# Bias rows two heads ahead on the ACT queue, and stores moved from POOL to ACT, in a two-layer decoder step

## The chip, the cores and the metric

One core of one Trainium2 chip runs the whole program. The metric is the device time in microseconds (us) of one execution, given as the median of several runs. Engines are named as in the profile: PE (TensorE matmul) and PEld (its weight load), DVE (VectorE), ACT (ScalarE), POOL (GpSimd), SP (SyncE, which here only issues DMAs). Each engine works through its own instructions in the order written. A DMA is issued by an instruction of SP, ACT or POOL; one that has to wait for data holds everything that is queued behind it on that engine.

## The reference, cut to what matters

One inference step of a two-layer decoder, on a prompt of 256 tokens and 8 samples of 8 tokens each (N = 320 columns), with width 2048, all in float32:

```python
# layer 0 (even): one input projection, two branches, one output projection
z = x @ w_in                               # 73 column tiles of 128
qa, ka, va, ga, qm, km, vm, om, gm, im, fm = split(z)
attn = moba(qa, ka, va, rel_bias)          # 8 heads of 128; prompt: causal softmax(q k^T*scale + T5 bias) v
                                           # samples: 16 cached pages of 128 keys each, top 3 blocks of 256 + own keys
hm, state = mlstm(qm, km, vm, im, fm)      # 4 heads of 256, matrix memory C, normaliser n, stabiliser m
x = layernorm(ALPHA*x + concat(attn*silu(ga), headnorm(hm)*sigmoid(om)*silu(gm)) @ w_out)
# layer 1 (odd): y = w_out(B * conv3(C * (w_in x)) * silu(G)), then layernorm again
```

Besides the two x, it returns the keys and values of layer 0 (`k_out`, `v_out`), the mLSTM's final states (`cp_out` for the prompt, `cs_out`, `n_out`, `m_out`) and the convolution's last rows. The T5 bias of a prompt head depends only on the distance between query and key.

## The kernel before, in words

All activations are kept transposed, 128 features by 320 columns. A projection tile is `lin`: 128 output columns, weights in two halves of 512 KB (`raw`, 11 buffers, loaded on SP at L226). ACT copies a half to float32r (`sh`) and DVE makes the remainder (`sl`, both by the helper at L202 to L204, recorded as L86); PE then does 24 matmuls per half from `sh` and `sl`. At most 4 halves are split ahead (`HL`). Attention over the cached pages uses the same `raw` buffers: each item loads two pages, one on SP and one on POOL (`k_load` L456, `v_load` L464), and goes to PE unsplit (`kv`).

The order of work is written out when the program is built. Items (weight halves, page pairs, mLSTM states) stand in one list: 8 page items, then 4 or 5 weight halves, and so on. Between matmuls, `stages()` steps four `Chain` queues of generators (A: sample softmax, B and E: prompt heads, values, mLSTM; C: gates) when a small model (`Plan`) says that the time has come. The model prices PE, ACT and DVE instructions, and no DMA issue.

Prompt attention, per head h: the key tile (`post_k`, L350) is evacuated by ACT (`kT`) and DVE (`ks`) and stored by two DMAs on POOL; the value tile (`post_v`, L359) is evacuated by ACT and stored by one DMA on POOL; then `prompt_head` (L404) is put on chain B (even h) or E (odd h). It loads `bt`, 128 rows of 256 bias values that are windows of the DRAM row `rel` (L406, on POOL), does the scores on PE, and DVE adds the bias (L413, L414). Row maxima on DVE, exponentials on ACT, a scaling on DVE and transposes on PE follow. `bt` has two buffers.

`rel` is made once by `bias_rows` (L324): one PE product, one DVE addition, one store on POOL (L330), and 8 small loads of `dt15` from it, on POOL too (L333).

The mLSTM (`mlstm_head`, L832, on chain B) reads weighted keys `ml.ks` and values `ml.vs` made by `k_natural` and `vm_natural`; these were written to DRAM (`kd`, `vd`) by 4 + 4 DMAs of POOL at L803 and L829 and are read back some hundred us later by `new_states` (L1252). `cp_out` is stored at L942 on POOL.

Of the kernel before, what the change touches and what calls it, by code (L numbers as in the profile page):

```python
# [18 lines left out]
F32 = mybir.dt.float32  # L19
# [9 lines left out]
T = 256  # L29
# [4 lines left out]
AH = 8  # L34
# [25 lines left out]
def _rev(ap, first, n):  # L60

    return bass.AP(tensor=ap.tensor, offset=ap.offset + first, ap=[list(ap.ap[0]), [-1, n]])
# [88 lines left out]
def trunk_kernel(ctx, tc, x_in, kc, vc, pages, cst_in, seg_in, hot_in, small_in, c0_in, n0_in, w_in,  # L151
                 y_out, k_out, v_out, cp_out, cs_out, n_out, m_out, conv_out):
    nc = tc.nc
# [4 lines left out]
    def mm(out, lhsT, rhs, tiles=1, **k):  # L158

        n = math.prod(rhs.shape[1:])  # L160
        cost = max(n * 1.68e-3, 0.21) if rhs.dtype == F32 else max(n * 0.46e-3, 0.11)
        plan.t -= 0.2
        plan.spend("pe", cost / tiles, 0.2)
        nc.tensor.matmul(out, lhsT=lhsT, rhs=rhs, **k)  # L164

    def transpose(out, in_, identity):
        plan.t -= 0.2
        plan.spend("pe", 0.22, 0.2)
        nc.tensor.transpose(out, in_, identity)  # L169
# [135 lines left out]
    ks = pa_.tile([128, AH, 64], F32, name="ks")  # L305
# [9 lines left out]
    p1_ = p1.__enter__()  # L315
    qT = M[:, 8:16, 0:T]
    kT = p1_.tile([128, AH, T], F32, name="kT")
# [4 lines left out]
    rel = dr.tile([8, 512], F32, name="rel")  # L322

    def bias_rows():  # L324
        r = b_bank()
        mm(r[:8, :512], lhsT=small[:32, S_REL:S_REL + 8], rhs=hot[:, :512], start=True, stop=True)
        yield HOLD
        row = early[:8, 1024:1536]
        dve.tensor_tensor(row, r[:8, :512], hot[:8, 512:1024], op=OP.add)
        nc.gpsimd.dma_start(rel, row)  # L330
        for hf in range(2):
            for j in range(4):
                nc.gpsimd.dma_start(dt15[32 * j:32 * j + 32, hf, :],  # L333
                                    bass.AP(tensor=rel.tensor, offset=rel.offset + 512 * (4 * hf + j) + 120,
                                            ap=[[0, 4], [1, 8], [1, 136]]))

        dve.tensor_tensor(om[:, 4:8], onb[:, 0:4], onb[:, 4:8], op=OP.add)
        dve.tensor_scalar(om[:, 4:8], om[:, 4:8], 1.0, -NEG, op0=OP.subtract, op1=OP.mult)
        yield
# [10 lines left out]
    def post_k(h):  # L350
        def f(p):
            act(kT[:, h, :], p[:, :T], AF.Copy)
            dve.tensor_copy(ks[:, h, :], p[:, T:])
            nc.gpsimd.dma_start(k_out[h][:, 0:T], kT[:, h, :])
            nc.gpsimd.dma_start(k_out[h][:, T:], ks[:, h, :])
            k_seen[0] += 1
        return f

    def post_v(h):  # L359
        def f(p):  # L360
            if h >= 2:
                B.until(f"v{h - 2}")
            v = p1_.tile([128, N], F32, name="vstage", tag="vstage", bufs=2)
            act(v, p, AF.Copy)
            nc.gpsimd.dma_start(v_out[h], v)
            B.add_urgent(f"v{h}", v_natural(h, v))
            (B, E)[h % 2].add(f"attn{h}", prompt_head(h, (b_bank, c_bank)[h % 2]))
        return f

    def v_natural(h, v):  # L370
        yield
        t = b_bank()
        transpose(t[:, 0:128], v[:, 0:128], ident)
        transpose(t[:, 128:256], v[:, 128:256], ident)
        transpose(t[:64, 256:384], v[:, 256:320], ident)
        yield HOLD
        c = slice(h * 128, h * 128 + 128)
        act(vp[:, :, h, :], t[:, :256].rearrange("p (j d) -> p j d", j=2), AF.Copy)
        dve.tensor_copy(vs[:, c], t[:64, 256:384])
        yield  # L380
# [15 lines left out]
    def post_ga(h):  # L396
        def g(p):
            sg = gate_tile()
            yield from sigmoid(p, sg)
            dve.tensor_tensor(M[:, h, :], p, sg, op=OP.mult)  # L400

        return lambda p: C.add(f"post{cga[h]}", g(p))

    def prompt_head(h, x_bank):  # L404
        bt = p1_.tile([128, 256], F32, name="bt", tag="bt", bufs=2)
        nc.gpsimd.dma_start(bt, bass.AP(tensor=rel.tensor, offset=rel.offset + 512 * h, ap=[[1, 128], [1, 256]]))  # L406
        s = x_bank()
        mm(s[:, 0:128], lhsT=qT[:, h, 0:128], rhs=kT[:, h, 0:128], start=True, stop=True)
        mm(s[:, 128:384], lhsT=qT[:, h, 128:256], rhs=kT[:, h, 0:256], start=True, stop=True)
        yield HOLD  # L410
        S = p1_.tile([128, 384], F32, name="pS", tag="pS", bufs=2)
        st4 = p1_.tile([128, 8], F32, name="st4", tag="st4", bufs=2)
        dve.scalar_tensor_tensor(S[:, 0:128], s[:, 0:128], SCALE, _rev(bt, 127, 128), op0=OP.mult, op1=OP.add)  # L413
        dve.scalar_tensor_tensor(S[:, 128:384], s[:, 128:384], SCALE, _rev(bt, 255, 256), op0=OP.mult, op1=OP.add)  # L414
        dve.tensor_reduce(st4[:, 0:1], S[:, 0:128], axis=AX.X, op=OP.max, negate=True)
        dve.tensor_reduce(st4[:, 1:2], S[:, 128:384], axis=AX.X, op=OP.max, negate=True)
        yield
        act(S[:, 0:128], S[:, 0:128], AF.Exp, bias=st4[:, 0:1], accum_out=st4[:, 2:3])
        act(S[:, 128:384], S[:, 128:384], AF.Exp, bias=st4[:, 1:2], accum_out=st4[:, 3:4])
        yield  # L420
        dve.reciprocal(st4[:, 4:6], st4[:, 2:4])
        dve.tensor_scalar(S[:, 0:128], S[:, 0:128], st4[:, 4:5], None, op0=OP.mult)
        dve.tensor_scalar(S[:, 128:384], S[:, 128:384], st4[:, 5:6], None, op0=OP.mult)
        yield
        t = x_bank()
        for j in range(3):
            transpose(t[:, j * 128:j * 128 + 128], S[:, j * 128:j * 128 + 128], ident)
        yield HOLD
        P = p1_.tile([128, 384], F32, name="pP", tag="pP", bufs=2)
        act(P, t[:, :384], AF.Copy)  # L430
        yield
        B.until(f"v{h}")
        o = x_bank()
        mm(o[:, 0:256], lhsT=vp[:, 0, h, :], rhs=P[:, 0:256], start=True, stop=False, skip_group_check=True)
        mm(o[:, 128:256], lhsT=vp[:, 1, h, :], rhs=P[:, 256:384], start=False, stop=True, skip_group_check=True)
        yield HOLD
        while f"post{cga[h]}" not in C.done:
            yield HOLD
        dve.tensor_tensor(M[:, h, 0:T], o[:, 0:256], M[:, h, 0:T], op=OP.mult)
        yield  # L440
# [198 lines left out]
    ml = ML()  # L639
    ml.states = -1  # L640
    ml.dec = pc.tile([128, 32], F32, name="dec")
    kd, vd = (dr.tile([BH, 4, 64, DK], F32R, name=n) for n in ("kd", "vd"))
# [144 lines left out]
    def k_natural(hd, kt):  # L787
        yield
        t = b_bank()
        for j, (c, n) in enumerate(TOK):  # L790
            transpose(t[:n, j * 128:j * 128 + 128], km[hd][:, kt, c:c + n], ident)
        yield HOLD
        c = slice(kt * 128, kt * 128 + 128)
        w = lambda j: ml.AT[:TOK[j][1], j, 4 + hd:5 + hd]
        act(ml.ks[:64, c], t[:64, 256:384], AF.Identity, scale=w(2))
        for j in range(2):
            act(ml.kw[:, j, c], t[:, j * 128:j * 128 + 128], AF.Identity, scale=w(j))
        yield HOLD
        dve.scalar_tensor_tensor(ml.ks[64:128, c], t[:64, 256:384], w(2), ml.ks[:64, c].bitcast(F32),
                                 op0=OP.mult, op1=OP.subtract)  # L800
        if kt == 1:
            for r in range(4):
                nc.gpsimd.dma_start(kd[hd, r], ml.ks[64 * (r // 2):64 * (r // 2) + 64, :])  # L803
        yield

    def post_vm(hd, kt):
# [8 lines left out]
    def vm_natural(hd, v, kt):  # L815
        yield
        t = b_bank()
        for j, (c, n) in enumerate(TOK):
            transpose(t[:n, j * 128:j * 128 + 128], v[:, c:c + n], ident)
        yield HOLD  # L820
        c = slice(kt * 128, kt * 128 + 128)
        act(ml.vs[:, 0, c], t[:64, 256:384], AF.Copy)
        act(ml.vn[:, 0:2, c], t[:, 0:256].rearrange("p (j c) -> p j c", j=2), AF.Copy)
        yield HOLD
        act(ml.vn[:64, 2, c], t[:64, 256:384], AF.Copy)
        dve.tensor_tensor(ml.vs[:, 1, c], t[:64, 256:384], ml.vs[:, 0, c].bitcast(F32), op=OP.subtract)
        if kt == 1:
            for r in range(4):
                nc.gpsimd.dma_start(vd[hd, r], ml.vs[:, r % 2, :])  # L829
        yield  # L830

    def mlstm_head(hd):  # L832
# [31 lines left out]
        if hd == BH - 1:  # L864
            nc.gpsimd.dma_start(n_out, ml.n0)
        B.done.add(f"qw{hd}")
        yield
        t = b_bank()
        for kt in range(2):
# [64 lines left out]
        cp = P2.tile([128, 2, 258], F32, name="cp", tag="hn")  # L934
        for kt in range(2):
# [3 lines left out]
            yield HOLD  # L939
            act(cp[:, kt, :], t[:, :258], AF.Copy)  # L940
            yield
        nc.gpsimd.dma_start(cp_out[hd], cp)  # L942
        yield

    def rsqrt_step(y, var, t):
# [699 lines left out]
```

## Time and profile before

| | before |
|---|---|
| median of 3 runs | 1482.01 us (1481.88 to 1488.57) |
| profiled execution | 1483.53 us, span 1481.9 us |
| PE busy | 1446.9 us, 98% of the span |
| DVE, ACT, POOL busy | 774.7, 599.7, 265.2 us |
| DMA | 356.45 MB, 241 GB/s over the span |

Layer 0's input projection with both attentions and the mLSTM takes the first 770 us or so; output projection, layer 1 and the closing norm take the rest. The page counts a matmul as busy from its issue to a modelled end, so PE at 98% is not PE at its full rate; PEclk is the share of the full clock (2.4 GHz) that was granted, the lower of the two levels being 1.2 GHz.

### The profile page before, as it was taken

What the parts mean: (1) busy time and instruction counts of PE and PEld (TensorE: products, weight loads), DVE (VectorE), ACT (ScalarE), POOL (GpSimd) and SP (SyncE); (2) the same over time, 40 slices, a digit from 0 to 9 for tenths busy, and PEclk for the clock granted to TensorE, in tenths of its full rate; (3) what the DMA queues carried; (4) which work ended last, traced back from release to release, by engine and by line L of the source; (5) the groups of instructions that cost most, each with busy time, mean ns of one, the idle gap of its engine ahead of it and who ended that gap; (6) DMA issues with size and microseconds to landing.
All of it is one profiled execution on the core that took longest, in us unless ns stands there. A gap on an engine that the chain in (4) does not pass through costs nothing.

```text
span 1481.9 us, 32269 instructions
## 1 busy us (share of the span) xinstructions
PE 1446.9 (98%) x11983; PEld 1376.5 (93%) x11983; DVE 774.7 (52%) x1296; ACT 599.7 (40%) x1124; POOL 265.2 (18%) x500
## 2 busy tenths in 40 slices
PE   9999998799999999999999999999999999999998
PEld 9799888798889789899899999999999999999998
DVE  5324424234333433433457766776776666666665
ACT  5335434234333343433455343444443334334344
POOL 1422212113212232222101025313110000000000
PEclk9999999899999999999999999999999999999999
DMA  9889878758999998998954657767665444444412
GB/s 358 308 306 346 295 274 293 260 198 286 343 323 338 333 344 286 353 335 275 367 221 160 197 164 221 230 227 230 208 217 171 153 143 144 154 143 159 147 41 71
DMA packets 134575, 356.45 MB, mean 241 GB/s; under 512 B 24453, under 2 KB 30854, under 8 KB 134418
## 3 DMA queue, kind: packets, MB, share of 16 engines
q1 hardware_dynamic: 94082, 258.53, 50.3%
q0 software_dynamic: 40336, 95.87, 18.9%
q8 instruction: 94, 1.54, 0.4%
q14 instruction: 63, 0.52, 0.1%
HBM read 337.31 MB, written 16.98 MB: 239 GB/s over the span
## 4 chain that ended last, share of the span: by engine, by line
PE 78%; DMA 8%; issue 6%; DVE 2%; POOL 2%; POOLq 1%; ACT 1%; SPq 0%; ACTq 0%; DVEq 0%
PE lin L164 67%; PE kv L164 6%; DMA raw<-w_all 4%; DMA bt<-rel 2%; PE mB L164 2%; PE mC L164 2%; DVE sl L86 1%; POOLq L454 1%; ACT sh L86 1%; PE mB L169 1%; DMA pt<-pages 1%; PE mA L169 0%; POOL raw L461 0%; POOL Xl L1263 0%; DVE M L86 0%
## 5 line engine op out<-in xcount | busy, mean ns | idle before, releaser
L86 DVE TENSOR_TENSOR sl<-raw,sh 128x1024 fp32r<-128x1024 f32 (+1 forms) x341 | 410.5, 1214 | 387.9 <-ACT sh L86 377.7
L164 PE MATMUL lin<-Xh,sh 128*128 128x320 f32 x1648 | 524.6, 318 | 3.3 <-DVE sg L86 2.0
L164 PE MATMUL lin<-Xh,sl 128*128 128x320 f32 x1648 | 511.9, 311 | 1.4 <-DVE sl L86 1.4
L164 PE MATMUL lin<-Xl,sh 128*128 128x320 f32 x1648 | 511.9, 311 | 0.0
L86 ACT ACTIVATE sh<-raw 128x1024 fp32r<-128x1024 f32 (+1 forms) x341 | 352.9, 1046 | 318.8 <-PE lin L164 118.0
L164 PEld LDWEIGHTS lin<-Xh,sh 128*128 128x128 f32 x1648 | 312.0, 189 | 15.7 <-issue 5.5
L164 PE MATMUL lin<-X2h,sh 128*128 128x322 f32 x1024 | 318.6, 311 | 0.0
L164 PE MATMUL lin<-X2l,sh 128*128 128x322 f32 x1024 | 318.0, 311 | 0.0
L164 PE MATMUL lin<-X2h,sl 128*128 128x322 f32 x1024 | 317.8, 310 | 0.0
L164 PEld LDWEIGHTS lin<-Xh,sl 128*128 128x128 f32 x1648 | 311.6, 189 | 2.0 <-DVE sl L86 1.9
L164 PEld LDWEIGHTS lin<-Xl,sh 128*128 128x128 f32 x1648 | 312.1, 189 | 0.9 <-DVE Xl L86 0.3
L164 PEld LDWEIGHTS lin<-X2l,sh 128*128 128x128 f32 x1024 | 193.9, 189 | 0.1
L164 PEld LDWEIGHTS lin<-X2h,sh 128*128 128x128 f32 x1024 | 192.9, 188 | 0.1
L164 PEld LDWEIGHTS lin<-X2h,sl 128*128 128x128 f32 x1024 | 192.6, 188 | 0.0
L461 POOL DMA_DIRECT2D raw<-kc x128 | 69.0, 539 | 209.5 <-PE kv L164 73.8
L469 POOL DMA_DIRECT2D raw<-vc x128 | 68.9, 539 | 206.7 <-PE kv L164 85.2
L164 PE MATMUL kv<-raw,qp 128*32 128x256 f32 x1024 | 61.5, 382 | 2.5 <-DMA raw<-kc 1.4
L164 PE MATMUL kv<-raw,PT 128*32 128x128 f32 x2048 | 61.0, 274 | 0.0
L164 PEld LDWEIGHTS kv<-raw,PT 128*32 128x32 f32 x2048 | 54.7, 110 | 5.5 <-issue 4.6
L164 PEld LDWEIGHTS kv<-raw,qp 128*32 128x32 f32 x1024 | 30.5, 110 | 25.0 <-issue 5.4
L1290 POOL DMA_DIRECT2D cs_o<-xr x32 | 17.7, 552 | 158.2 <-DVE xr L86 158.2
L1350 POOL DMA_DIRECT2D conv_o<-ncv x1 | 0.5, 539 | 218.3 <-ACT ncv L86 218.3
(313 smaller groups left out, 1105.2 us busy)
## 6 DMA issues: line engine op xcount, KB each, us to landing
raw<-w_all SPq DMA_DIRECT2D x335, 512.0 KB, 4.6
raw<-kc POOLq DMA_DIRECT2D x128, 256.0 KB, 5.8
raw<-kc SPq DMA_DIRECT2D x128, 256.0 KB, 6.2
raw<-vc SPq DMA_DIRECT2D x128, 256.0 KB, 5.9
raw<-vc POOLq DMA_DIRECT2D x128, 256.0 KB, 6.0
raw<-c SPq DMA_DIRECT2D x32, 256.0 KB, 6.7
xr<-c POOLq DMA_DIRECT2D x32, 256.0 KB, 4.8
cs_o<-xr POOLq DMA_DIRECT2D x32, 256.0 KB, 4.5
```

Of the source, the lines that this page charges most:

```text
L86: return fn(out, *a, **k)
L164: nc.tensor.matmul(out, lhsT=lhsT, rhs=rhs, **k)
L169: nc.tensor.transpose(out, in_, identity)
L454: return queue.value_load(pt[0:1, b * NPG + j:b * NPG + j + 1], min_val=0, max_val=NPOOL - 1)
L461: queue.dma_start(r[:, j, :], kc[bass.ds(n, 1), u.half].rearrange("o p f -> (o p) f"))
L469: queue.dma_start(r[:, j, :], vc[bass.ds(n, 1), :, 512 * u.half:512 * u.half + 512] .rearrange("o p f -> (o p) f"))
L1290: nc.gpsimd.dma_start(cs_out[hd, b], c)
L1350: nc.gpsimd.dma_start(conv_out, ncv)
```

## The change

`bias_load(h)` takes the place of the load at the head of `prompt_head`. The loads for heads 0 and 1 are issued at the end of `bias_rows`' DMAs; the load for head h + 2 is issued right after DVE's two additions of head h (which read the buffer that it overwrites). They are issued by ACT instead of POOL. The stores of keys, values and `cp_out` are issued by ACT too. The writes of `kd` and `vd` stay on POOL and move from the ends of `k_natural` and `vm_natural` to `mlstm_head`, behind the step that makes `qw`.

```diff
@@ bias_rows
+        for h in range(2):
+            bias_load(h)
@@ post_k, post_v
-            nc.gpsimd.dma_start(k_out[h][:, 0:T], kT[:, h, :])
-            nc.gpsimd.dma_start(k_out[h][:, T:], ks[:, h, :])
+            nc.scalar.dma_start(k_out[h][:, 0:T], kT[:, h, :])
+            nc.scalar.dma_start(k_out[h][:, T:], ks[:, h, :])
-            nc.gpsimd.dma_start(v_out[h], v)
+            nc.scalar.dma_start(v_out[h], v)
@@ prompt_head
+    bts = {}
+
+    def bias_load(h):
+        if h < AH:
+            bts[h] = p1_.tile([128, 256], F32, name="bt", tag="bt", bufs=2)
+            nc.scalar.dma_start(bts[h], bass.AP(tensor=rel.tensor, offset=rel.offset + 512 * h, ap=[[1, 128], [1, 256]]))
+
     def prompt_head(h, x_bank):
-        bt = p1_.tile([128, 256], F32, name="bt", tag="bt", bufs=2)
-        nc.gpsimd.dma_start(bt, bass.AP(tensor=rel.tensor, offset=rel.offset + 512 * h, ap=[[1, 128], [1, 256]]))
+        bt = bts.pop(h)
...
         dve.scalar_tensor_tensor(S[:, 128:384], s[:, 128:384], SCALE, _rev(bt, 255, 256), op0=OP.mult, op1=OP.add)
+        bias_load(h + 2)
@@ k_natural, vm_natural
-        if kt == 1:
-            for r in range(4):
-                nc.gpsimd.dma_start(kd[hd, r], ml.ks[64 * (r // 2):64 * (r // 2) + 64, :])
-        if kt == 1:
-            for r in range(4):
-                nc.gpsimd.dma_start(vd[hd, r], ml.vs[:, r % 2, :])
@@ mlstm_head
         B.done.add(f"qw{hd}")
+        for r in range(4):
+            nc.gpsimd.dma_start(kd[hd, r], ml.ks[64 * (r // 2):64 * (r // 2) + 64, :])
+            nc.gpsimd.dma_start(vd[hd, r], ml.vs[:, r % 2, :])
...
-        nc.gpsimd.dma_start(cp_out[hd], cp)
+        nc.scalar.dma_start(cp_out[hd], cp)
```

## Rows read from the trace of the kernel before

**Rows 1.** The page's chain that ended last, by line.
```profile
PE lin L164 67%; PE kv L164 6%; DMA raw<-w_all 4%; DMA bt<-rel 2%; PE mB L164 2%; PE mC L164 2%; DVE sl L86 1%; POOLq L454 1%; ACT sh L86 1%; PE mB L169 1%; DMA pt<-pages 1%; PE mA L169 0%; POOL raw L461 0%; POOL Xl L1263 0%; DVE M L86 0%
```

**Rows 2.** Busy time by stretch: length, PE, PEld, DVE, ACT, POOL, clock, DMA.
```profile
180.00:340.00 160.00, 142.19 (x1409) 131.73 (x1407) 56.72 (x107) 57.69 (x121) 34.94 (x65) 0.94 0.73 261
...
360.00:760.00 400.00, 395.32 (x4161) 356.07 (x4154) 154.90 (x312) 154.91 (x319) 97.34 (x181) 1.00 0.92 329
780.00:880.00 100.00, 100.00 (x682) 99.84 (x682) 71.39 (x109) 46.29 (x69) 9.12 (x23) 1.00 0.55 180
```

**Rows 3.** Waits of PE from 120 to 340 us: total, times, longest.
```profile
PE mB L169 <- DVE pS L86: 9.3, 1, 9.3
PE mC L169 <- DVE pS L86: 7.5, 2, 4.5
```

**Rows 4.** Waits of DVE in the same stretch.
```profile
DVE pS L86 <- DMA bt<-rel: 50.5, 7, 13.5
```

**Rows 5.** Chain of waits around the bias loads of heads 4 and 6: start, length, what.
```profile
225.32 4.64 DMA raw<-w_all
...
288.12 7.35 DMA bt<-rel
295.56 0.62 DVE pS L86 x2
...
297.97 0.95 PE mB L169 x3
```

**Rows 6.** The tile bt: issue duration (ns), first and last start; landing times.
```profile
L406 POOL DMA_DIRECT2D bt<-rel x8: 536/536/545, 121.2 to 322.7; - x8
L86 DVE SCALAR_TENSOR_TENSOR pS<-mB,bt x8: 283/352/415, 130.2 to 295.8; 128x128 f32<-128x128 f32 x4, 128x256 f32<-128x256 f32 x4
...
DMA to landing us min/median/max: 5.5/6.8/9.1
```

**Rows 7.** Busy time by stretch, where the granted clock was low.
```profile
180.00:200.00 20.00, 16.99 (x106) 16.43 (x104) 7.60 (x14) 7.26 (x16) 2.68 (x5) 0.91 0.75 270
...
260.00:300.00 40.00, 30.70 (x286) 29.27 (x286) 9.83 (x18) 10.04 (x20) 6.46 (x12) 0.84 0.64 234
300.00:320.00 20.00, 20.00 (x232) 18.59 (x232) 7.77 (x10) 7.52 (x11) 4.84 (x9) 0.91 0.60 204
```

**Rows 8.** Timeline of ACT, 42 us: the query copies of the first page unit.
```profile
42.46 0.35 ACT L86 ACTIVATE qp<-qs 128x32 f32<-128x32 f32 x2 [0.24 <-DVE qs L86]
```

**Rows 9.** Timeline of DVE, 43 us: the addition that makes the row rel.
```profile
43.42 0.67 DVE L86 TENSOR_TENSOR S<-mB,S 8x512 f32<-8x512 f32 x1
```

**Rows 10.** Chain of waits at 44 us.
```profile
44.38 2.10 DMA rel<-S
```

**Rows 11.** Timeline of PE: the first page bunch, and waits in the second.
```profile
44.55 3.66 PE L164 MATMUL kv<-raw,qp 128*32 128x256 f32 x64 [1.01 <-issue]
...
66.56 0.64 PE L164 MATMUL kv<-raw,qp 128*32 128x256 f32 x8 [0.79 <-DMA raw<-kc]
67.79 0.64 PE L164 MATMUL kv<-raw,qp 128*32 128x256 f32 x8 [0.59 <-DMA raw<-kc]
```

**Rows 12.** Timeline of SP: a lone issue, and seven stores issued one behind another.
```profile
11.53 0.31 SPq L1107 DMA_DIRECT2D pt<-pages  x1
...
1475.96 3.45 SPq L1522 DMA_DIRECT2D y_o<-M  x7
```

**Rows 13.** Timeline of POOL: a store of keys and a write of kd that waited.
```profile
309.47 0.54 POOL L354 DMA_DIRECT2D k_o<-kT  x1 [20.82 <-ACT kT L86]
...
562.94 1.07 POOL L803 DMA_DIRECT2D kd<-kws  x2 [8.49 <-ACT kws L86]
```

**Rows 14.** Timeline of DVE, then of ACT: qw of mLSTM head 0, next write of vms.
```profile
402.62 0.22 DVE L86 TENSOR_TENSOR qw<-qm,mB 128x64 f32<-128x64 f32 x1 [0.16 <-ACT dt L86]
...
467.35 0.27 ACT L86 ACTIVATE vms<-mB 64x128 fp32r<-64x128 f32 x1 [3.45 <-PE mB L169]
```

**Rows 15.** The page's groups of instructions: the splits of DVE and ACT.
```profile
L86 DVE TENSOR_TENSOR sl<-raw,sh 128x1024 fp32r<-128x1024 f32 (+1 forms) x341 | 410.5, 1214 | 387.9 <-ACT sh L86 377.7
L86 ACT ACTIVATE sh<-raw 128x1024 fp32r<-128x1024 f32 (+1 forms) x341 | 352.9, 1046 | 318.8 <-PE lin L164 118.0
```

## The prediction

> **What bounds the kernel now.** I read the chain of waits first. It runs through PE for most of the span, but one transfer stands in it that moves no weights: the bias rows, 2% of the span [rows 1]. The busy times by stretch say where that hurts. From 360 to 760 us PE is idle 400 - 395.32 = 4.68 us, from 780 to 880 us it is never idle; from 180 to 340 us it is idle 160 - 142.19 = 17.81 us, and the granted clock is 0.94 there against 1.00 in the others [rows 2]. So the first layer's prompt heads hold the only large loss. PE's own waits in that stretch name it: three times its transposes wait for DVE's `pS`, 9.3 + 7.5 = 16.8 us together [rows 3]. DVE in turn waited 50.5 us, at seven of the eight heads, for `bt` [rows 4]. The chain around head 6 shows the link: load issued at 288.12, DVE's addition at 295.56, PE's transposes at 297.97 [rows 5]. The load is issued only when its head begins and takes 5.5 to 9.1 us to land [rows 6], while the plan, which prices no DMA, has already put the transposes into PE's order.
>
> **Bias rows two heads ahead.** On one chain the additions of heads 0 and 6 start at 130.2 and about 295.5 us, so two heads lie some 55 us apart [rows 5, 6]. Issued right behind head h, a load that needs 5.5 to 9.1 us has landed long before head h + 2, even if the stretch shrinks by 20 us. The DVE wait goes for all seven heads. What is late next is PE's normal work: the stretch from 360 us on has the same mix of weights and pages without bias waits, and loses 4.68 us in 400, which is 1.9 in 160 [rows 2]. Idle time saved: 17.8 - 1.9 = 15.9 us. Its bounds are 0, if another wait takes all of it, and 17.8.
>
> The clock comes back too. Granted shares of 0.91, 0.84 and 0.91 over 20, 40 and 20 us [rows 7] lack 1.8 + 6.4 + 1.8 = 10 us of full clock, that is 20 us at 1.2 GHz instead of 2.4, each time around an idle PE. Where PE was idle at the low level it lost nothing more; if all idle time fell there, only 10 - 17.8/2 = 1.1 us of work was lost, if none did, 10. I take 6, near the middle, since the clock is still low in a stretch where PE is busy for all of its 20 us [rows 7].
>
> DMA must follow. The stretch moved 261 GB/s over 160 us, 41.8 MB. Pressed into 138 us that is 303 GB/s, below the 329 GB/s kept up from 360 to 760 us [rows 2], so I cost it at 1 us.
>
> **The first two loads.** They cost something. `bias_rows` is stepped before the first page unit's query copies, so on ACT the loads for heads 0 and 1 stand in front of the two `qp` copies that ran at 42.46 us [rows 8]. The loads read `rel`, which DVE makes at 43.42 [rows 9], and whose store lands at 44.38 + 2.10 = 46.48 [rows 10]. ACT is held until then, issues two DMAs and copies for 0.35 us. Behind it waits PE: the first 64 page matmuls started at 44.55 and need `qp` [rows 11].
>
> No DMA is issued by ACT in this trace. The nearest rows are SP's: 0.31 us alone, and 3.45/7 = 0.49 us in a row [rows 12]. I take 0.45, with 0.31 and POOL's 0.54 [rows 6] as ends. So PE starts at 46.48 + 0.9 + 0.35 = 47.7, which is 3.2 us later. The clock may dip behind that pause as it did near the others: 1.8 us at most, taken from the stretch at 180 [rows 7]; I take 1.5. In return, the second bunch of pages, for which PE waited 0.79 + 0.59 = 1.4 us [rows 11], has landed when PE comes to it, since POOL's loads don't hang on `qp`. Net cost 3.2 + 1.5 - 1.4 = 3.3 us, with bounds 0 and 5.
>
> A rule of the Trainium skill bears on the 0.45: Perfetto Trace Analysis, "DMA Instruction — HWDGE (DVE, Sync)", says that the sequencers issuing hardware-generated DMAs share one descriptor generator and wait for its lock. No run here shows it, as SP alone issues such DMAs. By it, each of the two loads could also wait out one of SP's issues, about 0.5 us each as an estimate from the rows above, and the forecast would be 1 us higher.
>
> **Stores and loads on ACT.** ACT issues 16 key stores, 8 value stores, 8 bias loads and 4 `cp_out`: 36 x 0.45 = 16.2 us. ACT is busy 154.91 of 400 us [rows 2], so most of it lies in idle time. The waits matter more. The second key store waits for DVE's `ks`, and the load for head h + 2 waits for DVE's additions of head h; behind them on ACT stand the splits `sh`, for these DVE's `sl`, and for that PE. With up to four halves split ahead, I cost this at 1 us; if the cover is gone, the bound is the second rival below. The value stores and `cp_out` wait for ACT's own copies only.
>
> **POOL.** It loses 36 issues of 0.54 us and waits such as the 20.82 us in front of a key store [rows 13]. The page loads behind these start earlier, but SP loads the other page of each pair and the buffers come free no sooner; apart from the 1.4 us counted above I give this nothing, with 0 and 2 us as bounds.
>
> **kd and vd.** The eight writes of a head move to where their data is long made, so waits such as 8.49 us [rows 13] leave POOL. The next head overwrites `vms` no sooner than 467.35, and the writes now start near 402.62 [rows 14]; eight issues of 0.54 us and a landing of some us fit into those 65 us. Cost and gain 0, within 1 us either way. `cp_out` likewise.
>
> **The sum**, against the profiled execution of 1483.53 us (span 1481.9, and 1.6 around it): -15.9 - 6 + 1 + 3.3 + 1 = -16.6, so 1466.9. The median of the runs shown lies 1.5 lower, at 1482.01; from it I forecast 1465 us, with 1460 to 1471 as the likeliest case's own range.
>
> **Rivals.**
> *Late weights take the wait's place.* Behind a bias wait the chain shows a weights load of 4.64 us whose slot had only been freed by DVE after that wait [rows 5]. If such a load, not the bias, is next at each of the three heads where PE stalled, 3 x 4.64 = 13.9 us of the gain come back: 1479 us. For it: DMA is near 92% later on. Against it: the slot comes free earlier when DVE isn't held.
> *ACT and DVE in lock step.* Slower. Eight bias loads and eight key stores hold ACT until DVE has caught up. Then a split starts only after the hold, and PE gets its half one ACT copy and one DVE remainder late: 1.046 + 1.214 = 2.26 us [rows 15], sixteen times 36 us. The time would be 1465 + 36 - 1 = 1500. It beats the gain once (16.6 + 1)/16 = 1.1 us of each hold reaches PE. For it: DVE's idle time is mostly a wait for `sh`, 377.7 us [rows 15]. Against it: up to four halves lie ready, and heads come some 27 us apart.
> *The loads come no earlier.* If ACT reaches them so late that DVE still waits, nothing is gained and the start costs 3.3: 1485 us. The 55 us between heads speak against it.
> *More than forecast.* The pause at 44 us is hidden and all 10 us of clock return: 1482 - 15.9 - 10 + 1 = 1457 us.
>
> **Chances.** Forecast 0.64, late weights 0.14, lock step 0.10, no earlier 0.04, more 0.08. The range from 1456 to 1480 takes in the first, the second and the last, at whose edges about 0.05 is left out, so some 0.8. A measurement can tell 0.5%, 7.4 us, from no change: under 1474.6 lie the forecast and the last case, 0.72; the late weights and the loads that come no earlier are within it, 0.18; lock step is slower, 0.10.
>
> **What would show it.** Right: no wait of DVE for `bt`, PE's waits for `pS` gone, a granted clock near 1 from 180 us to the end of the prompt heads, and PE idle there for some 2 to 4 us. At 44 us PE's first page matmuls start near 47.7. Wrong: these matmuls start at 44.6 (the first loads cost nothing); ACT's splits start behind a DMA issue while PE waits for `sl` (lock step); PE idle in the prompt heads behind `raw<-w_all` (late weights).

## The result, and the profile after

The changed kernel takes 1473.46 us (median of 15 runs, 1468.49 to 1478.43) against 1482.99 us (15 runs, 1477.92 to 1488.57) on the same chip, a ratio of 0.9932 with a 95% interval of 0.992 to 0.9944. It is 9.5 us faster, where 17 were forecast. The profiled execution took 1471.28 us, 12.25 less than that of before; the sum had 16.6.

The page's chain, first by engine and then by line, no longer holds a bias row; of its DMA share 2% are weights, and the pages of values and the load of `seg` now stand among its longest parts:

```profile
PE 88%; DMA 5%; issue 2%; DVE 2%; POOL 1%; ACT 1%; POOLq 0%; SPq 0%; ACTq 0%; DVEq 0%
PE lin L164 75%; PE kv L164 8%; DMA raw<-w_all 2%; PE mB L164 2%; PE mC L164 2%; PE mB L169 1%; PE mA L169 1%; DMA Xl<-kd 1%; DVE M L86 1%; DMA raw<-vc 1%; DMA pt<-pages 1%; POOL Xl L1269 1%; DVE sl L86 0%; DMA hn<-seg 0%; ACT sh L86 0%
```

Busy time by stretch (length, PE, PEld, DVE, ACT, POOL, granted clock, DMA share, GB/s), the first two stretches of [rows 2]:

```profile
180.00:340.00 160.00, 158.52 (x1612) 147.53 (x1612) 68.49 (x128) 67.55 (x144) 31.93 (x61) 1.00 0.83 300
360.00:760.00 400.00, 387.96 (x4028) 349.55 (x4027) 159.76 (x323) 156.62 (x318) 90.29 (x168) 0.99 0.89 316
```

From 180 to 340 us PE's idle time fell from 17.81 to 1.48 us and the clock is full, where [rows 7] had 0.84 to 0.91. From 360 to 760 us it rose from 4.68 to 12.04, and the clock is 0.99: there part of the gain went again.

The tile `bt`, as in [rows 6] (issue duration in ns, first and last start; landing):

```profile
L411 ACTq DMA_DIRECT2D bt<-rel x8: 332/332/450, 47.4 to 246.2; - x8
...
DMA to landing us min/median/max: 2.8/3.5/7.2
```

Waits of PE from 120 to 340 us and from 600 to 720 us (total, times, longest), the first in place of [rows 3]; DVE's wait for `bt` [rows 4] is gone:

```profile
PE mB L169 <- ACT dt L86: 1.4, 1, 1.4
...
PE kv L164 <- DMA raw<-vc: 4.3, 3, 2.6
PE lin L164 <- ACT sh L86: 1.7, 1, 1.7
PE lin L164 <- DVE sl L86: 0.7, 1, 0.7
```

**Where the time went.** PE runs the same 11983 matmuls in the same order in every kernel here. So the start of the n-th matmul can be compared between two traces, and the difference shows at which matmul time is won or lost. It is worked out from the starts of all matmuls, in us against the profiled execution of before; negative is earlier. The heads of the columns are the matmul's number and its start before; each row is one profiled execution. The rows below the first are runs 3, 1, 5, 6, 7, 8 and 10 of the next section.

| kernel (median, us) | 520 at 73 | 2950 at 354 | 3100 at 370 | 5700 at 624 | 5850 at 639 | 6590 at 704 | 6800 at 720 | 7400 at 797 |
|---|---|---|---|---|---|---|---|---|
| changed (1473.46) | 2.8 | -23.2 | -21.3 | -20.9 | -18.8 | -18.8 | -12.0 | -13.6 |
| bias rows alone (1461.6) | 2.4 | -22.2 | -22.2 | -22.9 | -23.0 | -23.0 | -23.0 | -23.0 |
| kd, vd back (1467.25) | 4.3 | -21.7 | -18.3 | -19.4 | -17.1 | -17.1 | -15.6 | -17.1 |
| kd, vd back, POOL shifted (1462.21) | 3.4 | -21.1 | -21.1 | -21.1 | -20.7 | -20.7 | -20.7 | -20.7 |
| the same with single rows (1466.4) | 0.9 | -25.1 | -20.2 | -19.8 | -17.5 | -17.5 | -16.2 | -17.8 |
| changed, POOL shifted (1470.38) | 3.1 | -22.2 | -22.2 | -22.4 | -22.3 | -22.3 | -17.3 | -18.9 |
| the same, kd, vd on ACT (1468.58) | 2.5 | -23.1 | -23.1 | -15.8 | -16.9 | -16.9 | -15.3 | -15.3 |
| kd, vd moved alone (1491.92) | 4.4 | 1.1 | 1.1 | 2.9 | 6.8 | 6.8 | 14.1 | 14.1 |

The prompt heads (columns 73 to 354) give 26.0 us in the changed kernel and 24.5 to 26.0 in every kernel with the bias rows ahead. The changed kernel then gives back 1.9 us near 354, 2.1 near 630 and 6.8 near 712. Two stretches of POOL stand behind the first of these and the last. In the first stretch, eight page loads and the load of `seg` (timeline: start, length, what, idle time before it and its releaser):

```profile
310.96 0.54 POOL L470 DMA_DIRECT2D raw<-kc  x1 [14.51 <-PE kv L164]
314.99 0.55 POOL L470 DMA_DIRECT2D raw<-kc  x1 [3.49 <-DVE M L86]
316.29 0.54 POOL L470 DMA_DIRECT2D raw<-kc  x1 [0.75 <-issue]
...
323.23 0.53 POOL L666 DMA_DIRECT2D hn<-seg  x1
```

The second load came 3.49 us after the first had been issued, its neighbours 0.75. The instruction named as releaser is not what it waited for: in the built program it waits for an earlier split of DVE, which ended 3 us before. DVE then waits 6.6 us for `seg`, and PE the 1.4 us for `dt` above:

```profile
DVE M L86 <- DMA hn<-seg: 6.6, 1, 6.6
```

In the second stretch, the last mLSTM head:

```profile
675.46 0.54 POOL L478 DMA_DIRECT2D raw<-vc  x1 [12.78 <-DVE sl L86]
678.72 0.54 POOL L868 DMA_DIRECT2D n_o<-n  x1 [2.72 <-DVE n L86]
679.25 0.55 POOL L871 DMA_DIRECT2D kd<-kws  x1
...
684.49 0.59 POOL L478 DMA_DIRECT2D raw<-vc  x1 [0.78 <-PE mB L164]
```

In the kernel before, the same two page loads stand with the store of `n` alone between them:

```profile
694.48 0.54 POOL L469 DMA_DIRECT2D raw<-vc  x1 [10.30 <-PE lin L164]
697.57 0.54 POOL L865 DMA_DIRECT2D n_o<-n  x1 [2.55 <-DVE n L86]
698.85 0.54 POOL L469 DMA_DIRECT2D raw<-vc  x1 [0.74 <-DMA raw<-vc]
```

They lie 4.4 us apart before and 9.0 after; the eight writes of `kd` and `vd` stand between. PE's wait of 4.3 us for `raw<-vc` is this.

The rest of the 6.8 us goes with the clock, and so does most of what is lost near 630. By stretch, for the changed kernel at these two places:

```profile
606.00:616.00 10.00, 8.19 (x46) 7.92 (x47) 8.56 (x19) 5.36 (x8) 3.25 (x6) 0.83 0.94 327
690.00:710.00 20.00, 15.67 (x192) 13.42 (x189) 7.75 (x13) 5.29 (x8) 5.55 (x11) 0.83 0.99 361
```

and for the kernel before, near 712:

```profile
705.00:725.00 20.00, 20.00 (x240) 18.16 (x239) 10.17 (x21) 7.83 (x12) 5.36 (x10) 1.00 1.00 368
```

A granted share of 0.83 over 20 us lacks 3.4 us of full clock, over 10 us 1.7, and PE was idle for part of that. Near 630 PE waits in both kernels: 1.7 us for `sh` and 0.7 for `sl` in the changed one, as above, 1.1 and 0.7 before, where the clock stayed at 1.00.

### The profile page after: what moved, and what is told of

Read it like the earlier page. It is cut to its first block, busy times and chain, and to the rows that moved or that the text cites. A ratio compares the mean times of both kernels' runs of the same rounds, so it can differ in the third digit from the quotient of the medians.

```text
span 1469.6 us, 32236 instructions
## 1 busy us (share of the span) xinstructions
PE 1442.4 (98%) x11983; PEld 1371.8 (93%) x11983; DVE 775.7 (53%) x1296; ACT 598.8 (41%) x1124; POOL 245.7 (17%) x464
## 4 chain that ended last, share of the span: by engine, by line
PE 88%; DMA 5%; issue 2%; DVE 2%; POOL 1%; ACT 1%; POOLq 0%; SPq 0%; ACTq 0%; DVEq 0%
PE lin L164 75%; PE kv L164 8%; DMA raw<-w_all 2%; PE mB L164 2%; PE mC L164 2%; PE mB L169 1%; PE mA L169 1%; DMA Xl<-kd 1%; DVE M L86 1%; DMA raw<-vc 1%; DMA pt<-pages 1%; POOL Xl L1269 1%; DVE sl L86 0%; DMA hn<-seg 0%; ACT sh L86 0%
## 5 line engine op out<-in xcount | busy, mean ns | idle before, releaser
L164 PEld LDWEIGHTS lin<-Xh,sh 128*128 128x128 f32 x1648 | 310.7, 189 | 16.6 <-issue 6.5
L86 ACT ACTIVATE sg<-sg 128x320 f32<-128x320 f32 x71 | 33.3, 469 | 12.3 <-DVE sg L86 10.7
```

Of the source, the lines that this page charges most:

```text
L86: return fn(out, *a, **k)
```

## The experiments

Eleven kernels ran, each timed 4 to 12 times beside the kernel before, whose medians were 1482.76 to 1482.96. The intervals of the ratios are about 0.2% wide to either side, some 3.5 us; where two kernels differ by less, the table above is what tells them apart, with one execution each.

**1. kd and vd back.** The changed kernel with the eight writes at their old places.

```diff
@@ mlstm_head (after q w)
-        for r in range(4):
-            nc.gpsimd.dma_start(kd[hd, r], ...)
-            nc.gpsimd.dma_start(vd[hd, r], ...)
@@ k_natural, vm_natural
+        if kt == 1:
+            for r in range(4):
+                nc.gpsimd.dma_start(kd[hd, r], ...)   # and vd likewise
```

> The changed kernel, with the writes of kd and vd back at the ends of k_natural and vm_natural. Theory 1, the burst: in the last mLSTM head POOL waits for n_o's data, then issues eight writes, and the page loads queued behind them come 4.5 us later than before, so that PE waits for pages at 695 to 700 us of the changed kernel's span. Then this kernel gains 6.8 us on the changed one (1473.5), some 1466.5, or 0.989 of the kernel before, and PE's wait for raw<-vc goes. Theory 2, starvation: the prompt heads run faster and leave less loaded in advance, so that DMA gives the time back later wherever it is tightest, whatever stands in POOL's queue. Then it stays within 1.5 us of the changed kernel, 1472 to 1475 (0.993 of before), and late stalls of some 7 us stay.

1467.25 us, 0.9892 (0.9871 to 0.9914). The loss near 712 falls from 6.8 to 1.5 us. The burst of writes costs 6.2 us here. In the other pairs of kernels that differ by it alone it costs 5.0 (runs 4 and 2), 8.2 (runs 5 and 7) and 9.0 us (run 10 and the kernel before): the sign holds, the size depends on the rest.

**2. The first two bias loads on POOL**, behind the loads of `dt15`; all else as changed.

```diff
-            bias_load(h)
+            bias_load(h, nc.gpsimd)
```

> The changed kernel, with the bias loads of heads 0 and 1 issued by POOL behind its dt15 loads; all else as changed. ACT is then not held for the store of rel, and PE's first page matmuls start at 44.6 us, not near 48. Theory 1: the net cost of that hold, 2.8 us in the two traces, comes back, 1470.7 or 0.9915 of before. Theory 2: time won early is given back late, so it stays at 1473.5 (0.993).

1469.84 us, 0.9912 (0.9892 to 0.9932). The time fits, but not for the reason given. ACT is no longer held, yet PE is as late after the second bunch (3.5 us at matmul 520, 2.8 in the changed kernel). What went is the loss near 354. With two more loads on POOL its 115th DMA is the last page load of a bunch (299.87 us); experiments 5 and 7 show why that matters.

**3. Bias rows alone.** The kernel before, with only the bias loads ahead and on ACT; stores, kd and vd as before.

> The kernel before with one part of the change: bias loads two heads ahead on ACT; stores and kd, vd as before. DVE's wait for bt (50.5 us) and PE's waits for pS (16.8 us) go as in the changed kernel. Theory 1: it carries the whole gain of 26 us minus the 2.8 at the start and has no burst: 1466 to 1468, 0.989 to 0.990. Key and value stores back on POOL cost 0 to 2 us of that. Theory 2: 1473.5 again (0.993), with stalls late in the stage.

1461.6 us, 0.9857 (0.9833 to 0.9881). This is faster than expected, and faster by 5.65 us than run 1, from which it differs by the stores alone. So moving the stores to ACT cost 5.65 us; the first theory had put a gain of 0 to 2 us there. The stretches of this run:

```profile
180.00:340.00 160.00, 159.14 (x1616) 148.11 (x1615) 68.28 (x129) 68.11 (x143) 39.39 (x75) 1.00 0.85 301
360.00:760.00 400.00, 394.35 (x4086) 357.03 (x4085) 160.45 (x324) 158.80 (x323) 89.83 (x167) 1.00 0.89 315
```

PE is idle 5.65 us in the second stretch (the same figure by chance), against 4.68 before and 12.04 in the changed kernel.

**4. Runs 1 and 2 together.**

> The changed kernel with both edits, kd and vd back and the first two bias loads on POOL. Theory 1: both gains add, 6.8 + 2.8 = 9.6 us, some 1464 or 0.987 of before. Theory 2: like the changed kernel, 1471 to 1474 (0.992 to 0.994).

1464.83 us, 0.9877 (0.9856 to 0.9897). As expected in size; it does not tell the causes apart.

**5. The place of POOL's stop.** In all traces POOL's queue stops for some 2.5 to 2.8 us now and then, and its DMAs can be counted: in the changed kernel at the 115th (314.99 us above), the 231st and the 344th, before the change at the 115th too, in front of a bias load:

```profile
251.28 0.55 POOL L406 DMA_DIRECT2D bt<-rel  x1 [2.51 <-issue]
```

Taking stores off POOL moves the stop to another transfer. This run is run 1 with two idle loads on POOL early on:

```diff
             k_seen[0] += 1
+            if k_seen[0] == 4:
+                junk = p1_.tile([128, 8], F32, name="junk", tag="junk")
+                for i in range(2):
+                    nc.gpsimd.dma_start(junk[:, 4 * i:4 * i + 4], ...)   # 128 rows of 4 floats of rel
```

> The kernel with the writes of kd and vd back at their old places (1467.25 us), plus two tiny loads (128 x 4 floats of the bias rows into a spare tile that nothing reads) on POOL's queue at 79 us. Phase theory: POOL's queue stops for about 2.6 us at every 115th DMA or so (the 115th, 230th, 344th of each run so far), and taking 20 stores off POOL moved the first stop to the second of the eight page loads ahead of the load of seg (issued 3.95 us after the one before, where its neighbours take 1.3). Two more DMAs put it on the last page load of the bunch before, near 298 us, where POOL idles 12 us anyway: the jump of 3.3 us at 334 falls under 1, the time to 1464 to 1465.5. Store theory (the stores cost what they cost through ACT's holds and the issue slots that ACT now shares with SP): nothing changes, 1466.5 to 1468, and the jump at 334 stays.

1462.21 us, 0.9857 (0.9834 to 0.988). Two more transfers make it 5.0 us faster. The 115th DMA is now the last page load of its bunch, ahead of a pause:

```profile
296.79 0.54 POOL L474 DMA_DIRECT2D raw<-kc  x1 [0.80 <-DVE sl L86]
300.68 0.55 POOL L474 DMA_DIRECT2D raw<-kc  x1 [3.35 <-DMA raw<-kc]
313.14 0.54 POOL L474 DMA_DIRECT2D raw<-kc  x1 [11.92 <-PE kv L164]
```

The loss near 354 is gone (3.4 to 0): in run 1 PE waits 1.2 us for `dt` there and the granted clock is 0.83 from 335 to 345 us; in this run PE has no such wait and the clock is 1.00. There the phase theory holds. The whole gain is larger than it had said. Near 630 the loss falls from 2.3 to 0.4, but this is not shown to be the stop's doing: PE waits there for `sh` and `sl` in both runs (1.7 and 0.7 us, 1.5 and 0.7), and what differs is the clock (run 1, then run 5):

```profile
606.00:616.00 10.00, 7.57 (x66) 6.86 (x59) 7.12 (x14) 5.39 (x8) 2.68 (x5) 0.83 0.93 328
```

```profile
606.00:616.00 10.00, 8.69 (x58) 8.43 (x59) 8.63 (x19) 4.75 (x8) 3.48 (x7) 1.00 0.90 299
```

Run 11, which has its stores on POOL, has 0.83 there too, from 602 to 612 us. Why the 1.5 us that run 1 loses near 712 goes as well is not shown either.

**6. Single rows.** The same two loads with one row of four floats each.

> As the run that put two tiny loads of 128 rows on POOL at 79 us (1462.21 us; without them 1467.25), but each load has one row of 4 floats. If POOL's stop comes after a count of DMA issues, it moves by two loads all the same, to the last page load of the bunch near 298 us: 1461 to 1464. If it comes after a count of rows (descriptors), two rows move nothing: the stop stays at the second load of the bunch near 315 us and the time at 1466.5 to 1468.

1466.4 us, 0.9893 (0.987 to 0.9915), and the stop stays at the second load of the late bunch, though that is now the 117th DMA:

```profile
309.14 0.54 POOL L474 DMA_DIRECT2D raw<-kc  x1 [14.75 <-PE kv L164]
313.12 0.55 POOL L474 DMA_DIRECT2D raw<-kc  x1 [3.44 <-DVE M L86]
```

So the stop does not come after a number of DMAs. It goes with the rows that they carry; bytes would hardly move it, since the loads of 128 rows have 2 KB beside 256 KB for a page. The added issues are the same in both runs, so run 5 gained nothing from the issues as such. Counted from the program, 13704 rows stand ahead of the first stop in all the other traces, whatever the mix of loads and stores, and 27024 to 27152 ahead of the second in the eight traces where it stands clear of other waits, while its number there runs from 230 to 235. What POOL does in the stop stays open.

**7. The changed kernel, shifted.** The loads of 128 rows in the changed kernel itself.

> The changed kernel (1473.46 us) with the same two tiny loads on POOL at 79 us; the burst of kd and vd stays. If the place of POOL's stop and the burst are two costs that add up, the two loads take away the 5 us that they took from the kernel without the burst (1467.25 to 1462.21): 1467.5 to 1470. If the stop matters only in the kernel without the burst (the burst hides it in the last state head), 1470 to 1472.5 from the 1.7 us at 334 alone.

1470.38 us, 0.9926 (0.9905 to 0.9946): 3.1 us faster than the changed kernel, in the second range and 0.4 us above the first. The two costs do not simply add: the place of the stop is worth 3.1 us here and 5.0 in run 5. The losses near 354 and 630 are gone; the one near 712 stays at 5.0, and PE's wait from 680 to 712 us with it:

```profile
PE kv L164 <- DMA raw<-vc: 3.1, 2, 2.0
```

**8. The burst on ACT's queue**, in the kernel of run 7.

```diff
-            nc.gpsimd.dma_start(kd[hd, r], ml.ks[...])
-            nc.gpsimd.dma_start(vd[hd, r], ml.vs[...])
+            nc.scalar.dma_start(kd[hd, r].bitcast(F32), ml.ks[...].bitcast(F32))
+            nc.scalar.dma_start(vd[hd, r].bitcast(F32), ml.vs[...].bitcast(F32))
```

> The run before last (the changed kernel with two tiny loads on POOL) with the eight writes of kd and vd of each state head, at the same place in the program, on ACT's queue instead of POOL's (32 writes in all). Queue theory (the page loads stand behind the burst and the store of n on POOL): the loss of some 6 us at the last state head goes and little takes its place, 5 to 7 us below the kernel with the burst on POOL, 1462 to 1465. Contention theory (the writes themselves fill the DMA engines while the pages of values are late): the same time as with the burst on POOL, within 1.5 us. Third: ACT's issues of 0.34 us, 2.7 a head, stand in front of the state products' steps on ACT, and the loss stays between.

1468.58 us, 0.9913 (0.9892 to 0.9934). The wait for `raw<-vc` near 712 is gone, and the next page load follows the store of `n` on POOL by 1.28 us, where it was 4.86 in run 7:

```profile
680.67 0.54 POOL L872 DMA_DIRECT2D n_o<-n  x1 [2.54 <-DVE n L86]
681.95 0.54 POOL L482 DMA_DIRECT2D raw<-vc  x1 [0.74 <-PE kv L164]
```

Five of the eight writes leave ACT just before, from 678.60 to 681.05 us; so it was the queue and not the writes' own traffic. Near 712 1.6 us are still lost; PE waits 1.3 us there for DVE's `dt`. And 7.3 us are lost elsewhere, between the columns at 370 and 624, most of them at 465 us. ACT's timeline there:

```profile
463.47 0.45 ACTq L875 DMA_DIRECT2D kd<-kws  x1
...
463.95 1.51 ACTq L876 DMA_DIRECT2D vd<-vms  x1
...
468.13 0.45 ACTq L876 DMA_DIRECT2D vd<-vms  x1
469.51 0.45 ACTq L875 DMA_DIRECT2D kd<-kws  x1
471.50 0.45 ACTq L876 DMA_DIRECT2D vd<-vms  x1
...
473.42 0.69 ACT L86 ACTIVATE O<-kv,rinv 128x512 f32<-128x512 f32 x1 [8.99 <-DMA kd<-kws]
```

and PE's wait for it, from 460 to 475 us:

```profile
PE mA L169 <- ACT O L86: 6.1, 1, 6.1
```

The clock falls behind that wait, to 0.78 from 475 to 485 us. Eight issues took ACT 9.9 us. Three of them start 0.02 to 0.03 us after the landing of a page load that SP had issued (468.11, 469.49, 471.47 us). In the built program the writes of ACT and the loads of SP take turns on eight completion counters, and each waits until the transfer ahead of it on its counter has landed. A burst on ACT therefore waits for SP's pages.

**9. Stores alone** moved to ACT, in the kernel before.

> The kernel before with only the stores of k, v and the final states moved to ACT; bias rows late and on POOL, kd and vd as before. Store theory: these stores cost 5.6 us wherever they are put (1467.25 against 1461.6), so 1487.5 to 1489.5. Phase theory: what they cost is 2.5 us at the first page matmuls (ACT waits with each store of the small half of a key row for DVE) and where POOL's stop of 2.6 us falls; here its 115th DMA is the third page load after 311 us, where the late bias rows leave slack: 1484 to 1486.

1478.45 us, 0.9965 (0.9952 to 0.9977): faster, outside both expectations. They had not reckoned with the bias loads, which still stand on POOL here and come earlier when fewer stores stand ahead of them. DVE's wait for them from 120 to 345 us, 50.5 us in seven waits before, is:

```profile
DVE pS L86 <- DMA bt<-rel: 33.6, 4, 11.0
```

That gain is contained in that of the bias rows, and the changed kernel can't have it twice: with the bias rows ahead, in runs 3 and 1, the same move costs 5.65 us.

**10. kd and vd alone** moved, in the kernel before.

> The kernel before with only the writes of kd and vd moved to the eight-write burst after q w. Burst theory: page loads of the last state head stand behind the burst and the store of n on POOL, 6 us as between 1473.46 and 1467.25: 1487 to 1490. Rival (the burst costs only together with the stores that left POOL, by the phase of POOL's stop): 1482 to 1484.

1491.92 us, 1.0056 (1.0034 to 1.0077). The burst theory's sign, 9 us slower than before, 2 above its range, and dearer than in the changed kernel: 7.3 us near 712 and 3.9 near 630, with a clock of 0.83 from 625 to 645 us. The page load behind the burst:

```profile
704.34 0.54 POOL L859 DMA_DIRECT2D n_o<-n  x1 [2.72 <-DVE n L86]
704.87 0.55 POOL L862 DMA_DIRECT2D kd<-kws  x1
...
710.04 0.59 POOL L469 DMA_DIRECT2D raw<-vc  x1 [0.86 <-PE mB L164]
```

**11. First two bias loads later.** Run 3, with these two issued from the third and fourth head of keys.

```diff
-        for h in range(2):
-            bias_load(h)
@@ post_k
+            if 3 <= k_seen[0] <= 4:
+                bias_load(k_seen[0] - 3)
```

> Bias rows ahead on ACT as the only change (1461.6 us), but the first two loads issued from the third and fourth head of keys, at about 68 and 79 us, when the bias rows have long been written. Theory: ACT is no longer held for the rows at 42 to 47 us, so the delay of 4.2 us at the first page matmuls, of which 2.4 come back at the second bunch, goes: 1459 to 1460.5. Rival: ACT waits there for something else that is late anyway (the key rows), and the time stays 1461 to 1462.5.

1461.38 us, 0.9855 (0.983 to 0.988), the rival's time, nothing gained, but not for its reason. ACT copies the queries at 42.97 us and PE runs the first 64 page matmuls in one go, but then waits for the second bunch of pages (ACT, then PE):

```profile
42.97 0.35 ACT L86 ACTIVATE qp<-qs 128x32 f32<-128x32 f32 x2 [0.24 <-DVE qs L86]
```

```profile
45.05 3.66 PE L164 MATMUL kv<-raw,qp 128*32 128x256 f32 x64 [1.18 <-issue]
...
66.45 1.27 PE L164 MATMUL kv<-raw,qp 128*32 128x256 f32 x16 [1.16 <-DMA raw<-kc]
68.63 0.91 PE L164 MATMUL kv<-raw,qp 128*32 128x256 f32 x8 [0.90 <-DMA raw<-kc]
```

**What the runs add up to.** 1482.99 - 21.4 (bias rows alone) + 5.65 (stores on ACT) + 6.2 (kd and vd) = 1473.46. This closes by construction, as each term is the difference of two neighbours in a row of kernels; in another order the terms differ, as runs 1, 7 and 9 show. Runs 3, 5 and 11 are the fastest of all and the same to within their intervals; run 3 is the simplest of them: bias rows ahead on ACT, nothing else.

## Why the prediction was half right

**Bias rows ahead: right.** The three terms -15.9 - 6 + 1 = -20.9 answer to 21.4 measured with this part alone. The idle time left was to be 1.9 us in 160 and is 1.48, the clock is back at 1.00, and the stretch moves 300 GB/s where 303 were reckoned. None of the rivals' waits took the place: no weights stand behind a bias wait any more, and PE's only wait from 120 to 340 us is the 1.4 us for `dt`, so no hold of ACT by a bias load or a store reaches it there.

**The first two loads: the mechanism right, the price not.** PE's pause is there. The forecast had the copies free PE at 47.7 us; in the changed kernel (PE, then ACT) it was 48.65, after 2.88 us of waiting:

```profile
45.13 0.64 PE L164 MATMUL kv<-raw,qp 128*32 128x256 f32 x8 [1.54 <-issue]
48.65 4.67 PE L164 MATMUL kv<-raw,qp 128*32 128x256 f32 x56 [2.88 <-ACT qp L86]
```

```profile
47.45 0.82 ACTq L411 DMA_DIRECT2D bt<-rel  x2
48.37 0.35 ACT L86 ACTIVATE qp<-qs 128x32 f32<-128x32 f32 x2 [5.58 <-DMA rel<-S]
```

But the pause costs nothing against the kernel without it (1461.6 and 1461.38). The return at the second bunch, put at 1.4 us, takes all of it: against run 11, PE in run 3 is 4 us late at the first bunch and level again after the second. The lateness of 2.8 us at matmul 520 is no price of the change: run 10, which changes nothing that early, has 4.4. The execution profiled before had an early start.

The two issues took 0.82 us together, where 0.9 was reckoned. The Trainium skill's rule on a shared generator of descriptors (Perfetto Trace Analysis, "DMA Instruction — HWDGE (DVE, Sync)") would have made it up to 1 us more; the trace shows no such wait there, but it is no test of the rule, since SP issued nothing from 46.15 to 49.80 us. One issue of run 8 took 1.51 us between issues of SP; what held it is not shown.

**Stores on ACT: the step that failed first.** It looked at ACT's holds, priced them at 1 us, and gave POOL's relief nothing, with 0 and 2 us as bounds. What counted was on POOL, and had the other sign: its queue stops for some 2.7 us every hundred or so page-sized transfers, and fewer stores ahead put the stop on the page loads in front of `seg`. Run 5 takes 5.0 of the 5.65 us away without touching a store; 3.4 us are seen behind those page loads in the traces, and what goes near 630 is the clock's and not shown to be the stop's. The trace of before had the stop, at 251.28 us, but the prediction does not name it.

**kd and vd: the step that failed by most.** Priced at 0 within 1 us, measured at 6.2. It asked when the data are made and when they are overwritten, and so found the writes free. It did not ask what stands behind the eight issues on POOL's queue: in the last mLSTM head page loads that PE needs at once. At the old places the writes waited too, 8.49 us in [rows 13], but then PE waited for no page: from 550 to 690 us it waited 2.8 us, all for `sh` and `sl`.

Together: of the 8.5 us between the forecast of 1465 and 1473.46, kd and vd make 6.2, the stores 4.65 beyond the 1 us priced, and the first loads -3.3; the bias rows make -0.5, and the remaining 1.4 us are that the median of before lies 1 us higher in these runs than in those that the forecast started from, and its rounding. The time lies 2.5 us above the 1460 to 1471 given to the likeliest case; it is inside the wider 1456 to 1480 by luck, since that was widened for late weights, which did not come.

## What to carry to other kernels

When a DMA moves on a queue, list what is issued behind it at its new place and when the consumer needs that; when its data are ready is only half the question. When DMAs leave a queue, look where that queue's periodic stop falls afterwards, by counting the rows it has issued in both traces. Read the granted clock next to each wait: behind a short wait it can cost as much again. And run the parts of a change apart: here one part was worth more alone than all together.

## What was not expected of the hardware

- POOL's DMA queue stops for 2.5 to 2.8 us beyond its usual spacing (issue gaps of 3.49, 3.35 and 3.44 us against 0.75 above), again and again, without any wait in the program that explains it; two added loads of 128 rows move the stop by two transfers, two of one row don't.
- The same load of 128 KB lands after 3.5 us on ACT's queue (2.8 to 7.2) and after 6.8 us on POOL's [rows 6]; its issue takes 0.33 us instead of 0.54. The two were not taken side by side: DMA's share from 180 to 340 us was 0.73 with POOL and 0.83 with ACT.
- Waits of much the same length near 630 (2.4 and 2.2 us) were followed by a granted clock of 0.83 in the changed kernel and run 1, and of 1.00 in run 5.
- Profiled starts vary: the same program was 4.4 us later after the second page bunch in run 10 than before. A loss of that size at one place needs a second trace.
